# A hybrid attention and mixture-of-experts layer: the first expert's rows selected by matmul, the router summed by quarters, the norm's scale and shift applied apart, the early weight slots split six and six

## The chip, the core and the metric

The kernel runs on one core of one Trainium2 chip, written in Bass with a tile framework whose scheduler sets the order of each engine's instructions. A core has TensorE (matmul, "PE" in the profile, with the load of its stationary operand as "PEld"), VectorE ("DVE"), ScalarE ("ACT"), GpSimd ("POOL") and SyncE ("SP", which here only issues DMAs), 16 DMA engines, SBUF (128 partitions) and PSUM (the matmul's accumulators). Each engine works through its own instructions in order, and semaphores tie them together. The metric is the device time of one execution in microseconds (us).

## What is computed

One layer on 512 tokens of width 1024, float32. The attention part ends in an output projection; the residual is normed, a router picks 4 of 32 experts for each token, the experts' outputs are added with their gates, and a second norm follows. The part of the reference that the change touches:

```python
x = _layer_norm(alpha * x + mix, ln1_g[l], ln1_b[l])       # mix: attention heads @ w_out
ffn = _moe(x, router_w[l], router_b[l], w_gate_up[l], b_gate_up[l], w_down[l], b_down[l])
x = _layer_norm(alpha * x + ffn, ln2_g[l], ln2_b[l])
...
def _layer_norm(x, g, b):                                   # (x - mu) * rsqrt(var + eps) * g + b
...
logits = (xf @ router_w + router_b)                         # in _moe
top_v, top_e = lax.top_k(logits, TOP_K)
gate_w = jax.nn.softmax(top_v, axis=-1)
...                                                         # per expert e, with its tokens' rows:
h = x_pad[tk] @ w_gu[e] + b_gu[e]
glu = gate * jax.nn.sigmoid(gate * SWIGLU_ALPHA)            # gate, up: clipped halves of h
y = ((up + 1.0) * glu) @ w_dn[e] + b_dn[e]
```

## The kernel before

**Weights of the experts.** Each expert has 12 pieces of 1 MB: eight of the gate-and-up matrix ("gu", one for each k of 128 input columns) and four of the down matrix ("dn"). `order` lists all 384; `fetch` (L78) brings the next one into a slot of the ring (tile `wring`). There are 18 slots in three pools, opened as SBUF comes free: `NA = (7, 3, 8)`. `prefetch` fills slots that have not been used yet; afterwards `ring` (L1110) issues the next fetch each time a piece is taken up, and that DMA waits until TensorE is done with what lay in the slot. All these DMAs stand in SP's queue.

**End of the attention part.** The output projection runs over four quarters q of 256 columns and four blocks t of 128 tokens (`product` L727, three matmuls for each pair of heads because the operands are split into a high and a low part). `residual` adds it to `x1all` and takes statistics. `turn` (L687) transposes two 128-column pieces of `x1all` for each quarter and block and copies them to `x1t`. In the last quarter `close(t)` takes the mean and the variance, and `router` (L698) makes the logits: eight matmuls `lp` from the eight stored pieces, corrected afterwards by the norm's factors (`fold`, L671, has folded the norm's scale and shift into the router's weights). `pick` (L831) finds the top four (`MAX8`, index, one-hot `oh`, sum `mf`, mask `msk`), TensorE counts the tokens ahead (`pp`), and `pos` gives each token's place in each expert's list. `norm` (L709) writes the normed block in place, each half either by ScalarE and two POOL instructions ("p") or by two VectorE instructions ("v"), and stores the block to DRAM (`x1d`), from where rows are gathered.

**From the list to the first matmul.** `routing.first` (L897) makes expert 0's list of row numbers: comparison of slot numbers with `pos` (`a0`), 12 small matmuls (`ip`), three VectorE instructions (`rows`). In `moe`, `gather` (L1007) clears the buffers `xg` and fetches an expert's rows from `x1d` by three indirect DMAs on POOL; `transposed` (L1015) turns them by TensorE to `xt`, six transposes and two copies. `gate_up` (L1042) multiplies them into the accumulator `gu`, after a bias matmul from `bpart`: for four pieces k the first two of three groups of 32 list places, then the third group of the same four, then the next four pieces. From expert 1 on the third group is skipped if the expert has at most 64 tokens. `act` is the activation (five instructions), `down` (L1079) the second matmul, after which ScalarE applies the gates and POOL adds the rows to `accd` in DRAM by indirect DMAs.

**Order of experts.** Before expert 0's matmuls the kernel gathers the rows of experts 0, 1 and 2 (`begin`, with `plan` making the lists of the next experts: `places` on VectorE, 12 small matmuls `ixp` for each expert). After them follow `start_sum` (the down biases weighted by the gates, 16 matmul instructions `ip` from `bd`, and the store of the scaled residual to `accd`) and `count`. Then, for each expert e: transposes of the previous expert's hidden rows (`at`), `gate_up` of e, transposes of the rows of e + 1, `down` of e - 1, `act` of e. The tail reads `accd` back, norms and stores.

## Time and profile before

| | |
|---|---|
| timed runs | 1452.08, 1453.5, 1456.73 us, median 1453.5 |
| profiled execution | 1447.06 us |
| its span, first to last instruction | 1445.3 us |
| mean granted TensorE clock | 0.968 |
| TensorE busy | 1303.5 us (90%) |
| VectorE, ScalarE, POOL busy | 413.2, 303.0, 391.4 us |
| moved by DMA | 454.17 MB, mean 314 GB/s |
| weight pieces | 384 of 1 MB, median 21 us from issue to landing |

Lines of code are those of the kernel before (L12 is line 12). A row in order of time gives the start, the length, the engine, the line, the operation, what is written "<-" from what is read, and how many like instructions the row merges; in brackets stands the idle time of the engine ahead of it and what ended that. The granted clock is a share of 2.4 GHz: 1.00 is that, 0.50 is 1.2 GHz. The DMA share is the mean busy share of the 16 DMA engines; it can come out a little above one.

### The profile page before, as it was taken

Reading aid. Unit: us, or ns where it says so; the run is one execution under the profiler, and the core shown is the slowest. Engines: PE = TensorE matmul, PEld = TensorE weight load, DVE = VectorE, ACT = ScalarE, POOL = GpSimd, SP = SyncE. Lnnn points to the kernel's source line nnn. Section 1 sums busy time; section 2 is a strip of 40 time slices with the busy share of each in tenths; the row PEclk is TensorE's granted clock in tenths of the full one; section 3 lists DMA queues with packets and bytes.
Section 4 is the critical chain, followed back from the end, with each engine's and each line's share of the span. In section 5 each row is a group of like instructions: output and inputs, shape, how many; then the busy total and the mean of one; then the engine's idle time right before and its main releaser. Section 6 shows DMA issues by size and latency. Waiting matters only on the chain. (4 is left out here: it accounts for less than half of the span.)

```text
span 1445.3 us, 31835 instructions
## 1 busy us (share of the span) xinstructions
PE 1303.5 (90%) x13903; PEld 672.3 (47%) x13904; DVE 413.2 (29%) x888; ACT 303.0 (21%) x683; POOL 391.4 (27%) x331
## 2 busy tenths in 40 slices
PE   8999899994999999899999999999899898998980
PEld 6777667893243443444343343444334333344340
DVE  3576464647212212222121212122121212001114
ACT  4475265641011011111111111111111111101111
POOL 5333333335103132132221213132331313131124
PEclk9999999996899999999999999999999999999996
DMA  8210113546889999999999999999999999999973
GB/s 220 81 34 1 48 44 124 205 161 253 314 317 393 371 396 403 400 405 406 399 410 401 407 392 408 405 401 402 393 403 397 399 397 409 392 402 386 407 256 127
DMA packets 126260, 454.17 MB, mean 314 GB/s; under 512 B 21416, under 2 KB 53642, under 8 KB 93334
## 3 DMA queue, kind: packets, MB, share of 16 engines
q1 hardware_dynamic: 107526, 435.00, 76.4%
q0 software_dynamic: 18432, 16.84, 5.6%
q8 instruction: 126, 2.06, 0.6%
q14 instruction: 32, 0.26, 0.0%
q10 hardware_dynamic: 144, 0.00, 0.0%
HBM read 441.26 MB, written 18.87 MB: 318 GB/s over the span
## 5 line engine op out<-in xcount | busy, mean ns | idle before, releaser
L1048 PE MATMUL gu<-wring,xt 128*32 128x512 f32 x5312 | 588.8, 595 | 16.9 <-DMA wring<-in_w_gate_up_dram 10.5
L1048 PEld LDWEIGHTS gu<-wring,xt 128*32 128x32 f32 x5312 | 181.3, 110 | 398.7 <-issue 351.2
L1087 PE MATMUL ya<-wring,at 128*32 128x256 f32 x5312 | 312.9, 387 | 8.0 <-DMA wring<-in_w_down_dram 3.6
L1104 POOL DMA_INDIRECT accd<-y,ix x96 | 151.1, 1574 | 487.6 <-ACT y L1103 464.4
L1070 DVE TENSOR_SCALAR ga<-gu 128x768 f32<-128x768 f32 x32 | 30.6, 958 | 778.5 <-PE gu L1048 506.7
L1087 PEld LDWEIGHTS ya<-wring,at 128*32 128x32 f32 x5312 | 171.1, 111 | 138.4 <-issue 35.4
L1010 POOL DMA_INDIRECT xg<-x1d,ix x96 | 101.6, 1058 | 327.9 <-PE ya L1087 156.2
L1021 ACT COPY xt<-tp 128x512 f32<-128x512 f32 x64 | 27.6, 482 | 562.9 <-PE gu L1048 304.7
L173 POOL TENSOR_TENSOR wl<-raw,wh 128x1024 fp32r<-128x1024 f32 (+2 forms) x28 | 67.9, 2430 | 94.8 <-ACT wh L170 91.2
L1103 ACT ACTIVATE y<-ya,gw 128x256 f32<-128x256 f32 x96 | 38.6, 473 | 209.9 <-PE ya L1087 123.4
L1020 PE MATMUL tp<-ident,ga 128*128 128x128 f32 x192 | 34.1, 291 | 40.5 <-DVE ga L1076 38.6
L880 DVE TENSOR_TENSOR places<-slot,pos 128x1536 bf16<-128x1536 bf16 x31 | 54.3, 1753 | 54.6 <-PE ixp L890 54.6
L1021 ACT COPY at<-tp 128x512 f32<-128x512 f32 x64 | 30.2, 481 | 133.2 <-PE tp L1020 133.2
L244 PE MATMUL pjt<-xh,wh 128*128 128x512 f32 (+1 forms) x136 | 52.8, 388 | 0.8 <-DVE xl L222 0.8
L1020 PEld LDWEIGHTS tp<-ident,ga 128*128 128x128 f32 x192 | 21.9, 143 | 68.1 <-issue 68.1
L244 PE MATMUL pjt<-xh,wl 128*128 128x512 f32 (+1 forms) x136 | 52.4, 385 | 0.0
L244 PE MATMUL pjt<-xl,wh 128*128 128x512 f32 (+1 forms) x136 | 52.1, 383 | 0.0
L170 ACT CAST wh<-raw 128x1024 fp32r<-128x1024 f32 (+2 forms) x28 | 29.5, 1054 | 52.9 <-issue 23.5
L1074 ACT ACTIVATE sg<-ga 128x768 f32<-128x768 f32 x32 | 27.0, 845 | 41.4 <-DVE ga L1070 37.8
L430 ACT ACTIVATE pr<-pr,nm 128x256 f32<-128x256 f32 (+3 forms) x64 | 33.8, 529 | 7.5 <-DVE nm L429 6.9
L1020 PE MATMUL tp<-ident,xg 128*128 128x128 f32 x192 | 28.8, 286 | 6.6 <-DMA xg<-x1d,ix 6.6
L1048 PE MATMUL gu<-bpart,bsel 96*32 96x512 bf16 x332 | 29.7, 389 | 3.5 <-DVE up L1072 3.2
(324 smaller groups left out, 1320.4 us busy)
## 6 DMA issues: line engine op xcount, KB each, us to landing
wring<-in_w_gate_up_dram SPq DMA_DIRECT2D x256, 1024.0 KB, 21.1
wring<-in_w_down_dram SPq DMA_DIRECT2D x128, 1024.0 KB, 21.4
raw<-in_w_in_dram SPq DMA_DIRECT2D x16, 512.0 KB, 3.9
raw<-in_w_out_dram SPq DMA_DIRECT2D x8, 512.0 KB
x1all<-in_x_dram SPq DMA_DIRECT2D x4, 512.0 KB, 7.6
x1d<-x1all SPq DMA_DIRECT2D x4, 512.0 KB
accd<-x1all SPq DMA_DIRECT2D x4, 512.0 KB
x1all<-accd SPq DMA_DIRECT2D x4, 512.0 KB, 6.4
```

Source lines behind the costliest of these rows:

```text
L173: eng.tensor_tensor(l[:, :m], raw[:, :m], h[:, :m].bitcast(FT), op=OP.subtract)
L244: nc.tensor.matmul(ps[:, qs], a[:, k, :], b[:, k, qs], start=(k == 0 and n_ == 0), stop=(k == 7 and n_ == 2))
L430: nc.scalar.activation(pr[:, :n], pr[:, :n], AF.Exp, bias=nm, scale=-1.0, accum_out=den)
L880: ins = self.nc.vector.tensor_tensor(a, self.slot[:, None, :].to_broadcast([P, n, NG * P]), pos[:, :, None].to_broadcast([P, n, NG * P]), ...
L1010: nc.gpsimd.indirect_dma_start(out=xg[:, g * 256:(g + 1) * 256], out_offset=None, in_=x1d, in_offset=bass.IndirectOffsetOnAxis(ap=ix[g], a ...
L1020: nc.tensor.transpose(pt[:, u * P:(u + 1) * P], src[:, (a + u) * P:(a + u + 1) * P], ident)
L1021: nc.scalar.copy(dst[:, a:a + n], pt[:, :n * P].rearrange("p (u q) -> p u q", q=P))
L1048: nc.tensor.matmul(ps[SL * c:SL * (c + 1), g, :], lhs(g), w[:, c * 512:(c + 1) * 512], start=start, stop=stop)
L1070: nc.vector.tensor_scalar(ga, v[:, :, :, 0], 7.0, None, op0=OP.min)
L1087: nc.tensor.matmul(ya[SL * c:SL * (c + 1), g, :], listed(at, k, g), w[:, k % 2, c * 256:(c + 1) * 256], start=(k == 0 and g % 2 == 0), sto ...
L1103: nc.scalar.activation(y[:, cs], ya[:, g, :], AF.Copy, scale=gw[g])
L1104: sc.append(nc.gpsimd.indirect_dma_start(out=accd, out_offset=bass.IndirectOffsetOnAxis(ap=ix[g], axis=0), in_=y[:, cs], in_offset=None, b ...
```

## The change

1. **Slots.** `NA = (6, 6, 6)`: still 18 slots, but 12 of them open before the last quarter. Attention's probability tiles move out of the pool `work` into pools of their own (`heads`), which are closed after the attention heads, so the second ring pool has room for six. The first six pieces are fetched ahead of the loads of the gate biases, six more in two lots of three in quarters 1 and 2, the last six after the last product.
2. **Router by quarters.** `turn` multiplies its two transposed pieces at once into a PSUM tile `lp` that all quarters share; `fold` therefore runs before the projection. `router` only reads the sum.
3. **Norm apart.** ScalarE writes (x - mean) / deviation for both halves; scale and shift follow as two instructions for each half on POOL or VectorE (`scaled`, `NORM1`), after the selection has read the block.
4. **First expert's rows.** `pick` makes a one-hot `oh0` of token against place for expert 0; `select` multiplies it with the normed block, eight matmuls for each block into two PSUM tiles. The result is already transposed; `first_rows` applies scale and shift in eight ScalarE instructions and writes `xt`. `routing.first`, expert 0's gather and its transposes are gone. All four blocks are stored to `x1d` after block 3 is scaled.
5. **Expert 0's matmuls** go piece by piece with all three groups, and the lists of experts 0 to 3, the gathers of experts 1 and 2, `start_sum` and `count` are put between the pieces.
6. **Later experts.** The transposes of the hidden rows stand in the middle of the next expert's `gate_up` instead of ahead of it.

```diff
-NA = (7, 3, 8)
-EARLY = (2, 1, 1)
-MORE = 1
+NA = (6, 6, 6)
+NORM1 = ["pp", "pp", "pv", "vv"]
...
-            pr = work.tile([P, S], FT, name="pr", tag="pr", bufs=6)
+            pr = hpool.tile([P, S], FT, name="pr", tag="pr", bufs=6)
...
+    env["prefetch"](NA[0])
     for i in range(NT):
         k0 = max(0, i - 1) * P
...
     swa.close()
+    heads.close()
     env["ring_pool"](NA[1])
...
     def turn(t, q):
...
-        nc.scalar.copy(x1t[t][a][:, k0:k0 + 2], pt[:, :256].rearrange("p (k q) -> p k q", k=2))
+        x1t = work.tile([P, 2, P], FT, name="x1t", tag="x1t", bufs=2)
+        nc.scalar.copy(x1t, pt[:, :256].rearrange("p (k q) -> p k q", k=2))
+        for k in range(2):
+            nc.tensor.matmul(lp[:, t, :NE], x1t[:, k, :], rw[:, 2 * q + k, :], start=(t == q == k == 0),
+                             stop=(q == 3 and k == 1), skip_group_check=True)
...
+    def select(t):
+
+        if t == 0:
+            picked.extend(psum.tile([P, 4, CAP], FT, name="sel", tag="sc", bufs=3) for _ in range(2))
+        for k in range(8):
+            nc.tensor.matmul(picked[k // 4][:, k % 4, :], x1all[:, t, k * P:(k + 1) * P], routing.oh0[:, t, :],
+                             start=(t == 0 and k % 4 == 0), stop=(t == NT - 1), skip_group_check=True)
+
+    def first_rows(xt):
+
+        for k in range(8):
+            nc.scalar.activation(xt[:, k % 2::2, SL * (k // 2):SL * (k // 2 + 1)],
+                                 picked[k // 4][:, k % 4, :].rearrange("p (g s) -> p g s", g=NG), AF.Identity,
+                                 scale=gbT[:, 0, k:k + 1], bias=gbT[:, 1, k:k + 1])
+
+    def scaled(t):
         for a in range(2):
             v = x1all[:, t, a * S:(a + 1) * S]
...
+            eng = nc.gpsimd if NORM1[t][a] == "p" else nc.vector
+            eng.tensor_tensor(v, v, gb[0][a], op=OP.mult)
+            eng.tensor_tensor(v, v, gb[1][a], op=OP.add)
...
+    def close(t):
+        turn(t, 3)
...
+        router(t, rs)
+        for a in range(2):
+            v = x1all[:, t, a * S:(a + 1) * S]
+            nc.scalar.activation(v, v, AF.Identity, bias=rs[:, 1:2], scale=rs[:, 0:1])
+        select(t)
+        if t < NT - 1:
+            scaled(t)
+
+    fold()
...
-        if q == 1:
-            env["prefetch"](NA[0])
-        if q == 2:
-            env["prefetch"](NA[1], True)
-            fold()
+        if q in (1, 2):
+            env["prefetch"](NA[1] // 2, True)
...
                 if t == NT - 1:
-                    mixs.close()
                     late.close()
+                    xgb = env["token_pool"]()
                     env["ring_pool"](NA[2])
-                    env["prefetch"](EARLY[0])
+                    env["prefetch"](NA[2], True)
                 if t > 0:
                     close(t - 1)
             close(NT - 1)
-            routing.first(rsm, psum)
+            first_rows(xgb[0].rearrange("p (a q) -> p a q", a=6))
+            scaled(NT - 1)
+            for t in range(NT):
+                nc.sync.dma_start(env["x1d"].rearrange("(s c) d -> s (c d)", c=NQ)[t * P:(t + 1) * P, :],
+                                  x1all[:, t, :])
             routing.gates_of(rsm, work)
...
-        self.places(self.a0[t // 2][:, t % 2:t % 2 + 1], self.pos[:, 0, t:t + 1])
+            self.oh0 = work.tile([P, NT, CAP], FT, name="oh0", tag="q32", bufs=2)[:, :]
+        nc.vector.tensor_scalar(self.oh0[:, t, :].rearrange("p (g s) -> p g s", g=NG),
+                                self.slot.rearrange("p (g c s) -> p g c s", g=NG, c=NQ)[:, :, 0, :],
+                                self.pos[:, 0, t:t + 1], mf[:, 0:1], op0=OP.is_equal, op1=OP.mult)
...
-        for k0 in (0, 4):
+        step = 1 if more is None else 4
+        for k0 in range(0, 8, step):
...
             groups(more, full, lambda: [rows(w, k, range(2, NG)) for k, w in ws.items()])
+            between.get(k0 + step - 1, lambda: None)()
...
-    begin(0)
-    begin(1)
-    begin(2)
...
-    hid = act(gate_up(transposed(xgs.pop(0), "xt", 1), ring("gu", 0), bsel[:, 0:1]))
-    start_sum(start)
-    count()
+    hid = act(gate_up(xgb[0].rearrange("p (a q) -> p a q", a=6), ring("gu", 0), bsel[:, 0:1], None,
+                      {1: lambda: begin(1), 3: lambda: (plan(0), begin(2)), 5: lambda: (start_sum(start), count())}))
...
-        at = transposed(hid, "at", 2)
         if e < NE:
+            at = []
...
-            ps = gate_up(xt, ring("gu", e), bsel[:, e:e + 1], more[e])
+            ps = gate_up(xt, ring("gu", e), bsel[:, e:e + 1], more[e],
+                         {3: lambda: at.append(transposed(hid, "at", 2))})
```

How the order of instructions changes, at three places. First TensorE in the last quarter, around the end of block 2's products (`op`): `pt` are the transposes of block 1, `pp` the count for block 0 and then block 1, `lp` the logits of block 1. Before:

```order
L733 MATMUL op<-wl,mnh 128x256
L733 MATMUL op<-wh,mnl 128x256
L695 MATMUL pt<-ident,x1all 128x128 x2
L847 LDWEIGHTS us
L847 MATMUL pp<-msk,us 128x32
L701 MATMUL lp<-rw,x1t 128x32 x6
L847 LDWEIGHTS on
```

and now:

```order
L866 LDWEIGHTS us
L866 MATMUL pp<-msk,us 128x32
L747 MATMUL op<-wh,mnl 128x256
L747 MATMUL op<-wh,mnh 128x256
L747 MATMUL op<-wl,mnh 128x256
L747 MATMUL op<-wh,mnl 128x256
L700 MATMUL pt<-ident,x1all 128x128 x2
L720 MATMUL sel<-oh_3602,x1all 128x96 x8
L704 MATMUL lp<-rw,x1t 128x32 x2
L866 LDWEIGHTS on
```

The count of block 0 stands ahead of the last products of block 2 instead of behind them, the selection of block 0 is new, and two logits matmuls are left of eight.

Second, TensorE through expert 0's matmuls with the weights (`gu<-wring`); `gp` and `ip` belong to the sum of the down biases, `cp` to the count, `tp` are transposes of gathered rows. Before, from the last list to the sum:

```order
L890 MATMUL ixp<-val,places 128x5
L1020 MATMUL tp<-ident,xg_3866 128x128 x6
L952 MATMUL gp<-ident,gd 128x128
L1048 MATMUL gu<-wring,xt 32x512 x32
L1048 LDWEIGHTS bsel
...
L1048 MATMUL gu<-wring,xt 32x512 x64
L959 MATMUL ip<-bd,gt 128x512 x3
```

and now, from the last list to the rows of expert 1:

```order
L908 MATMUL ixp<-val,places 128x5
L1052 MATMUL gu<-wring,xg_3733 32x512 x16
L957 MATMUL gp<-ident,gd 128x128
L1052 MATMUL gu<-wring,xg_3733 32x512
L964 MATMUL ip<-bd,gt 128x512 x8
L975 LDWEIGHTS on
L975 MATMUL cp<-msk,on 128x32
...
L1052 MATMUL gu<-wring,xg_3733 32x512 x23
L1023 MATMUL tp<-ident,xg_3734 128x128 x6
```

The six transposes ahead of the first weight matmul are gone, and lists, sum and count now stand between the weight matmuls instead of ahead of and behind them.

Third, SP's queue from the tenth piece (before) or the twelfth (now) to the first pieces that need a used slot. Before:

```order
L85 DMA wring<-in_w_gate_up_dram 128x2048 x3
L719 DMA x1d<-x1all 128x1024 x2
L85 DMA wring<-in_w_gate_up_dram 128x2048 x2
L719 DMA x1d<-x1all 128x1024
L85 DMA wring<-in_w_gate_up_dram 128x2048
L719 DMA x1d<-x1all 128x1024
L85 DMA wring<-in_w_gate_up_dram 128x2048 x2
L1130 DMA markd<-xg_3866 1x8
L85 DMA wring<-in_w_gate_up_dram 128x2048
L85 DMA wring<-in_w_down_dram 128x2x1024
L944 DMA bd<-in_b_down_dram 32x512 x8
L85 DMA wring<-in_w_down_dram 128x2x1024 x3
```

and now:

```order
L84 DMA wring<-in_w_gate_up_dram 128x2048 x3
L803 DMA x1d<-x1all 128x1024
L84 DMA wring<-in_w_gate_up_dram 128x2048 x4
L84 DMA wring<-in_w_down_dram 128x2x1024 x2
L803 DMA x1d<-x1all 128x1024 x3
L949 DMA bd<-in_b_down_dram 32x512 x8
L84 DMA wring<-in_w_down_dram 128x2x1024 x2
L84 DMA wring<-in_w_gate_up_dram 128x2048 x4
```

The last six slots stand together behind the store of block 0, and the other three stores behind them; the marker DMA that waited for the first gather is gone.

## Rows read from the trace of the kernel before

**Rows 1.** Windows: stretch, length, busy time of each engine, TensorE clock, DMA share, GB/s.

```profile
307.00:341.00 34.00, 27.78 (x230) 27.12 (x229) 22.15 (x75) 11.76 (x30) 16.18 (x11) 0.91 0.33 122
341.00:364.00 23.00, 6.24 (x78) 3.56 (x82) 16.05 (x39) 1.39 (x4) 11.40 (x10) 0.50 0.73 260
364.00:410.00 46.00, 45.74 (x336) 14.62 (x332) 10.96 (x29) 3.75 (x6) 5.98 (x6) 0.87 0.75 277
410.00:1390.00 980.00, 915.01 (x11028) 389.19 (x11020) 167.35 (x230) 115.02 (x240) 228.09 (x174) 0.99 1.02 399
```

**Rows 2.** SP's queue, waits: who waited for what, us in total, times, longest.

```profile
SPq L85 <- DMA wring<-in_w_gate_up_dram: 221.1, 117, 4.3
SPq L85 <- DMA wring<-in_w_down_dram: 193.2, 90, 3.7
```

**Rows 3.** Order of time, SP's queue, 220 to 560 us: start, length, DMA issued, count.

```profile
250.27 0.40 SPq L605 DMA_DIRECT2D raw<-in_w_out_dram  x1
251.10 4.17 SPq L85 DMA_DIRECT2D wring<-in_w_gate_up_dram  x5
...
284.41 0.98 SPq L85 DMA_DIRECT2D wring<-in_w_gate_up_dram  x2
...
297.84 1.37 SPq L85 DMA_DIRECT2D wring<-in_w_gate_up_dram  x3
...
331.04 1.71 SPq L85 DMA_DIRECT2D wring<-in_w_gate_up_dram  x2
...
408.00 1.19 SPq L85 DMA_DIRECT2D wring<-in_w_gate_up_dram  x2
```

**Rows 4.** Order of time, TensorE, 318 to 420 us.

```profile
318.90 1.42 PE L701 MATMUL lp<-rw,x1t 128*128 128x32 f32 x12
...
325.93 0.18 PE L847 MATMUL pp<-msk,us 128*128 128x32 bf16 x1 [2.03 <-DVE msk L844]
...
332.22 0.38 PE L695 MATMUL pt<-ident,x1all 128*128 128x128 f32 x2
...
348.89 1.04 PE L1048 MATMUL gu<-bpart,bsel 96*32 96x512 bf16 x8 [0.26 <-DVE v L874]
350.96 0.48 PE L890 MATMUL ixp<-val,places 128*128 128x5 bf16 x12 [1.03 <-DVE places L880]
...
362.82 0.66 PE L1020 MATMUL tp<-ident,xg 128*128 128x128 f32 x2 [5.11 <-DMA xg<-x1d,ix]
...
363.62 9.65 PE L1048 MATMUL gu<-wring,xt 128*32 128x512 f32 x64
...
387.16 1.98 PE L959 MATMUL ip<-bd,gt 32*128 32x512 f32 x6
...
399.78 7.07 PE L1048 MATMUL gu<-wring,xt 128*32 128x512 f32 x64
```

**Rows 5.** Order of time, VectorE, 295 to 420 us.

```profile
321.39 0.75 DVE L717 SCALAR_TENSOR_TENSOR x1all<-x1all,mv,gb 128x512 f32<-128x512 f32 x1
...
335.91 1.53 DVE L717 SCALAR_TENSOR_TENSOR x1all<-x1all,mv,gb 128x512 f32<-128x512 f32 x1
...
342.73 0.21 DVE L851 COPY pos<-pp 128x32 f32<-128x32 f32 x1
342.98 0.56 DVE L880 TENSOR_TENSOR a<-slot,pos 128x384 bf16<-128x384 bf16 x1
...
344.76 0.16 DVE L911 TENSOR_TENSOR ix<-inv,v 128x3 int32<-128x3 f32 x1
```

**Rows 6.** Order of time, POOL, 290 to 470 us.

```profile
335.43 1.46 POOL L715 TENSOR_TENSOR x1all<-x1all,gb 128x512 f32<-128x512 f32 x1
...
350.97 2.73 POOL L1010 DMA_INDIRECT xg<-x1d,ix  x1 [0.18 <-POOL xg L1005]
```

**Rows 7.** Order of time, ScalarE, 268 to 312 us.

```profile
283.50 1.05 ACT L170 CAST wh<-raw 128x1024 fp32r<-128x1024 f32 x1 [2.03 <-PE op L733]
...
298.87 0.37 ACT L696 COPY x1t<-pt 128x256 f32<-128x256 f32 x1
```

More of the change, by code (lines that the diff above doesn't have):

```diff
@@ L101, in x1_pool, with token_pool @@
                 p.tile([G, NE], BF, name="bsel"))
+    def token_pool():
+        p = ctx.enter_context(tc.tile_pool(name="xgp", bufs=1, side="left", reuse_waits="tile"))
+        return [p.tile([P, 768], FT, name=f"xg{i}") for i in range(3)]
     def prefetch(n=NE, pin=False):
@@ L494, in attention @@
     nsx.close()
+    mix_fs = late.enter_context(tc.tile_pool(name="mix_fs", bufs=1, side="right", reuse_waits="tile"))
+    hpool = pool(heads, "heads")
     fox = ExitStack()
@@ L683, in fold @@
         nc.vector.tensor_tensor(rw, rw, gbT[:, 0, :, None].to_broadcast([P, 8, NE]), op=OP.mult)
[L685 removed]
+    lp = psum.tile([P, NT, P], FT, name="lp", tag="ot", bufs=1)
     def turn(t, q):
[L688 to L691 removed]
         pt = psum.tile([P, S], FT, name="pt", tag="pt")
@@ L698, in router @@
     def router(t, rs):
-        lp = psum.tile([P, S], FT, name="lp", tag="sc", bufs=3)
-        for k in range(8):
-            nc.tensor.matmul(lp[:, :NE], x1t[t][k // 4][:, k % 4, :], rw[:, k, :], start=(k == 0), stop=(k == 7))
         lg = small.tile([P, NE], FT, name="lg", tag="lg")
         nc.vector.scalar_tensor_tensor(lg, rsum, rs[:, 1:2], rb, op0=OP.mult, op1=OP.add)
-        nc.vector.scalar_tensor_tensor(lg, lp[:, :NE], rs[:, 0:1], lg, op0=OP.mult, op1=OP.add)
+        nc.vector.scalar_tensor_tensor(lg, lp[:, t, :NE], rs[:, 0:1], lg, op0=OP.mult, op1=OP.add)
@@ L980, in count @@
         nc.vector.tensor_scalar(thr, cnt, float(2 * SL), None, op0=OP.is_gt)
-    bases = [1] + list(range(2, NE, 2))
-    ixs, gwt = ({0: [v[:, 0, g:g + 1] for g in range(NG)]} for v in (routing.ix0, routing.gw0))
+    bases = [0, 1] + list(range(2, NE, 2))
+    ixs, gwt = {}, {}
     def plan(e0):
@@ L1000, in plan @@
             gwt[e0 + e] = [gw[:, e, g:g + 1] for g in range(NG)]
-    xgb = []
-    for i in range(3):
-        xb = rt.tile([P, 768], FT, name=f"xg{i}")
-        nc.gpsimd.memset(xb, 0.0)
-        xgb.append(xb)
+    for i in (1, 2):
+        nc.gpsimd.memset(xgb[i], 0.0)
     def gather(ix, i):
@@ L1040, in groups, with gate_up @@
                 part()
-    def gate_up(xt, weights, pick, more=None):
+    def gate_up(xt, weights, pick, more=None, between={}):
         ps = gups
@@ L1054, in rows @@
             column_tiles(lambda g: listed(xt, k, g), w, False, k == 7, gs)
-        for k0 in (0, 4):
+        step = 1 if more is None else 4
+        for k0 in range(0, 8, step):
             ws = {}
             def full():
-                for k in range(k0, k0 + 4):
+                for k in range(k0, k0 + step):
                     ws[k] = weights(k).rearrange("p a c -> p (a c)")
@@ L1146, in moe @@
             more[e] = third(e)
-            ps = gate_up(xt, ring("gu", e), bsel[:, e:e + 1], more[e])
+            ps = gate_up(xt, ring("gu", e), bsel[:, e:e + 1], more[e],
+                         {3: lambda: at.append(transposed(hid, "at", 2))})
             if e + 1 < NE:
                 xt = transposed(xgs.pop(e + 1), "xt", 1)
-        down(at, ring("dn", e - 1), ixs[e - 1], gwt[e - 1], more.pop(e - 1, None))
+        else:
+            at = [transposed(hid, "at", 2)]
+        down(at[0], ring("dn", e - 1), ixs[e - 1], gwt[e - 1], more.pop(e - 1, None))
         if e < NE:
```

80 lines of the change are left out of this document (18 added, 62 removed).

## Prediction

> **What bounds the kernel now.** I first read the table of stages. From 410 to 1390 us the DMA share is 1.02 at 399 GB/s: for two thirds of the span the 16 DMA engines never rest [rows 1]. The waits of the queue that issues the weight slots agree: SP held a slot back 207 times, 414 us in all, because earlier slot transfers were still under way [rows 2]. TensorE is busy for 915 of those 980 us, close, but it is not what sets the pace. So the end is the moment at which the weight stream becomes continuous, plus a fixed amount of weight, plus a tail that the change leaves alone. A slot costs about 2.74 us: 358 of the 384 are issued between 408.00 and the end of that stretch (982 / 358) [rows 1, 3].
>
> Then I looked at what makes the stream start late. From 307 to 341 us the DMA share is 0.33, from 341 to 364 it is 0.73, from 364 to 410 it is 0.75 [rows 1]. The last two are 6.2 + 11.5 = 17.7 us of idle DMA. All ten early slots are issued by 297.84, the other eight follow from 331.04 on, and then the ring is full: a further transfer needs a slot that TensorE has used up. The first weight matmul runs at 363.62, 31.4 us behind the last product of the output projection (332.22), and the first slot that expert 1 frees goes out at 408.00, another 44.4 us later [rows 3, 4]. In between stands the detour of expert 0's rows: index list ready at 344.76 [rows 5], gather issued at 350.97 [rows 6], its last piece transposed at 362.82 after a wait of 5.11 us [rows 4]. The change replaces exactly this detour, so I cost it as a shift of the first weight matmul.
>
> **Step 1: TensorE up to the last product (332.22 now).** The logits' matmuls of the first three quarters move ahead: 3 quarters x 4 blocks x 2 = 24, in two passes each, 48 instructions. Twelve of these took 1.42 us [rows 4], 0.118 each: +5.7 us. TensorE fills this stretch completely (the output projection runs without holes), so it is paid in full. Blocks 0 and 1 need 12 fewer each in the last quarter: 24 x 0.118 = -2.8. The row selection of blocks 0 and 1 is new: 2 x 8 matmuls in two passes, 32 instructions; the trace has no such shape, the nearest are the logits (0.118) and the transposes (2 in 0.38): +3.8, and twice that at the low clock. The wait of 2.03 us for block 0's mask [rows 4] now has 16 product matmuls in front of it: I take half of it away, -1.0. Each early logits pair waits for a ScalarE copy of 0.37 us [rows 7], and at about six of the twelve places only one to four products stand between: 6 x 0.3 = +1.8. Sum +7.5: the last product ends near 339.7 (bounds 336, if copies and mask are hidden, and 343, if selection runs at half clock).
>
> **Step 2: from the last product to the first weight matmul (31.4 us now).** The chain to the last block's positions stays: 342.73 - 332.22 = 10.5 [rows 4, 5]; its logits are 12 instructions shorter per block, up to -2.8. Behind it come one multiply or add of block 2's half on VectorE, which now stands between the positions and the one-hot (0.75, as the row at 321.39), the one-hot itself (about 0.25, a quarter of the columns of the 0.56 us row at 342.98, plus fixed cost), the last selection (16 x 0.118 = 1.9, or 3.8 at the low clock; the clock was 0.50 over 341 to 364, so I take 3.0) and the bias matmuls (1.04). ScalarE's eight scalings (0.37 each as the copy) run half beside the selection and half beside the bias. Sum 10.5 + 0.75 + 0.25 + 3.0 + 1.04 = 15.5, less half a us for the shorter logits: 15. Bounds: 12.3 and 18.7. First weight matmul at 339.7 + 15 = 354.7, which is 8.9 earlier (bounds 15.3 and 1.9).
>
> A half that VectorE does while POOL does the other one can be slow. The same kind of VectorE instruction took 0.75 us at 321.39 and 1.53 at 335.91, where POOL had begun its 1.46 us instruction at 335.43 [rows 5, 6]. The Trainium skill (SBUF — State Buffer, Who interferes with whom) says that a VectorE instruction with two SBUF inputs and a GpSimd instruction that reads SBUF lock each other out, "whoever issues first gets the shared pair for the whole instruction"; the two rows agree. The change puts such a pair exactly there: both halves of block 2 are released by the same selection. If POOL wins, two VectorE instructions wait some 0.8 us each and the gain is 1.5 us smaller; that lies within the bounds above.
>
> **Step 3: from there to the stream.** Before, 44.4 us passed to the first slot of expert 1. Now TensorE also makes four index lists in this time, 0.48 each [rows 4]: +1.9; the six transposes of the hidden rows leave it, about -1.0; and the bias of expert 1 follows the last matmul of expert 0 at once, where the activation's two reads hold it up: 0 to 2, I take 0.5. The sum over the down biases (within the 12.6 us from 387.16 to 399.78) moves between two matmuls of expert 0 and costs the same. Net +1.4, so the shift that reaches the stream is 8.9 - 1.4 = 7.5; with the clock already raised by the selection it may be 8. I take **8**.
>
> Does the DMA keep up? At about 340 it owes six slots (16.4 us), the stored rows and the down biases (2.6 MB, 6.6 us at 399 GB/s): done near 363, when expert 0 has begun to free slots. It frees them one by one, 24 matmuls of 0.11 each (64 in 7.07 us), 2.65 us a slot against 2.74: the stream follows. Before expert 1's first four slots a hole of some 5 us is left (11.5 now). So the stream is still led by TensorE there, and the shift is what counts, not the whole 17.7.
>
> **What costs nothing, and its cover.** The first six slots stand ahead of the gate biases on SP: those are due at the bias matmuls (348.89), far behind. The third load of the output weights (250.27 now) falls behind a bias load that waits for the moved fold; its cast is at 283.50 [rows 3, 7], some 10 us of cover after it lands; without them it would hold the second half of a quarter. The store of block 0 stands on SP ahead of the last six slots; it needs POOL's four instructions after the first selection, about 339, when the last product frees the room anyway. Those slots are the third half-dozen: expert 0's eight are in the first twelve. Rows of experts 1 and 2 are gathered beside expert 0's matmuls; they are due after about 30 us. The fold moves, its price doesn't. From expert 4 on TensorE's order is as it was.
>
> **The sum.** The profiled execution took 1447.06 us (span 1445.3): 1447.1 - 8 = 1439.1. The three timed runs lie 6.4 us higher (median 1453.5); the same shift gives **1445.5**.
>
> **The rivals.**
> *More* (0.16): selection and logits fall into waits that TensorE has anyway, and the clock holds. First weight matmul at 336 + 12.3 = 348.3, 15.3 earlier, less 1.4: about 1439.5. For it: 2.03 us of waiting and a clock of 0.91 in 307 to 341. Against: the products before that run without a gap.
> *Too little to see* (0.24): selections at half clock, VectorE locked out, casts ahead of the copies: 342 + 17.2 = 359.2, 4.4 earlier, less 1.4: 1450.5.
> *Slower* (0.10): TensorE works in order, so a late ScalarE copy now holds the products behind each early logits pair, and ScalarE does the gate-bias casts in the same stretch. If each of the twelve pairs waits 1.6 us instead of the 0.15 in my sum, step 1 grows by 17: 1453.5 + 9 = 1462.5. It decides from 0.8 us each on (gain gone); slower than 0.3% from 1.2 on. Against it: the order puts 4 to 11 products behind most pairs.
> *The shift is not passed on* (in the 0.24): if the stream were held by something other than freed slots after 364, it would not move. Against it: its DMA idles there.
>
> **How the numbers follow.** Forecast 0.50, with its own range 1441 to 1449. The measurement tells about 0.3% (4.4 us) from no change: forecast and "more" are faster, 0.66; too little 0.24; slower 0.10. Low end 1437 holds most of "more"; the high end 1453 takes in "too little" and leaves the slow case out.
>
> **What would show it.** Right: first weight matmul near 355; no gather before it; the low-DMA stretch ends with the last product and the share from 341 to 400 is above 0.9; expert 1's first freed slot near 400; 1.02 after that. Step 1 is wrong if the last product of the projection is not near 340 (see TensorE's waits for ScalarE copies); step 2 if the first weight matmul is not 15 us behind it; step 3 if matmuls of expert 0 wait for index lists, gathers or weights. The whole is wrong if the continuous stretch has another rate than 399 GB/s.

## The result and the profile after

The changed kernel takes 1460.3 us (median of 18 runs, 1455.6 to 1471.2), the kernel before 1452.1 (18 runs, 1446.9 to 1458.5): ratio 1.0066, 95% interval 1.0044 to 1.0088. It is 8 us slower, where 8 us less were forecast. Ratios here and below are taken over the fast runs, and are not quotients of the medians. The profiled execution took 1456.1 (span 1454.4), 9.1 more than that of before.

The stages of the changed kernel, answering [rows 1] (stretch, length, busy time of PE, PEld, DVE, ACT and POOL, TensorE clock, DMA share, GB/s):

```profile
307.00:341.00 34.00, 30.26 (x251) 29.35 (x251) 16.47 (x49) 13.13 (x28) 11.32 (x8) 0.99 0.41 156
341.00:364.00 23.00, 17.66 (x90) 14.60 (x93) 12.05 (x42) 7.10 (x19) 7.55 (x6) 0.50 0.89 333
364.00:410.00 46.00, 44.87 (x393) 14.99 (x389) 24.37 (x52) 3.85 (x6) 9.28 (x9) 0.96 0.72 269
410.00:1390.00 980.00, 913.35 (x10956) 398.50 (x10949) 168.04 (x230) 115.33 (x240) 231.76 (x174) 0.98 1.02 397
```

The waits of SP's queue in the long stretch, answering [rows 2], and TensorE's and VectorE's waits that grew:

```profile
SPq L84 <- PE gu L1052: 167.2, 51, 9.9
SPq L84 <- PEq L1042: 156.4, 31, 11.2
SPq L84 <- PE ya L1093: 146.1, 34, 14.1
SPq L84 <- DMA wring<-in_w_gate_up_dram: 131.6, 73, 3.2
SPq L84 <- DMA wring<-in_w_down_dram: 102.9, 47, 3.7
...
PE gu L1052 <- DVE up L1078: 12.7, 19, 2.2
...
DVE ix L916 <- DMA accd<-y,ix: 180.8, 13, 15.2
```

The same views of before, beside the two lines of [rows 2]:

```profile
SPq L85 <- PE gu L1048: 101.0, 40, 10.3
SPq L85 <- PE ya L1087: 83.3, 32, 11.4
SPq L85 <- PEq L1039: 76.1, 18, 11.5
...
PE gu L1048 <- DVE up L1072: 3.2, 15, 0.2
```

Before, SP held slots back 414 us for DMAs and 260 for TensorE; now it waits 234 us for DMAs and 470 for TensorE, which frees the slots late. The last line of the first table is new: VectorE's write of an index list waits 180.8 us for a scatter.

**Two losses.** In the stage ahead of the stream the gain is smaller than forecast. TensorE, answering [rows 4]:

```profile
247.10 0.33 PE L747 MATMUL op<-wh,mnh 128*128 128x256 f32 x1
...
331.59 2.02 PE L720 MATMUL sel<-oh,x1all 128*128 128x96 f32 x16
...
339.63 0.18 PE L866 MATMUL pp<-msk,us 128*128 128x32 bf16 x1 [3.73 <-DVE msk L863]
340.53 3.73 PE L720 MATMUL sel<-oh,x1all 128*128 128x96 f32 x16
...
344.54 0.41 PE L747 MATMUL op<-wh,mnl 128*128 128x256 f32 x1
...
356.23 3.70 PE L720 MATMUL sel<-oh,x1all 128*128 128x96 f32 x16 [2.72 <-DVE oh L873]
361.42 1.04 PE L1052 MATMUL gu<-bpart,bsel 96*32 96x512 bf16 x8 [1.49 <-ACT xg L726]
362.22 2.92 PE L1052 MATMUL gu<-wring,xg 128*32 128x512 f32 x16
```

The last product runs at 344.5 (forecast 339.7, bounds 336 to 343), the first weight matmul at 362.2 (forecast 354.7), only 1.4 us before its old time. A part of this is not the change: the projection's first product comes 2.1 us later in this execution. In the profile of before it is this one:

```profile
245.03 0.33 PE L733 MATMUL op<-wh,mnh 128*128 128x256 f32 x1
```

From the projection's first product to the first weight matmul it takes 115.1 us, 118.6 before: 3.5 less. One execution of each is a coarse measure of that. Run 3 below, the kernel before with an edit behind this stretch, takes 123.3; runs 1, 2, 7, 8, 9 and 16, the changed kernel with edits behind it or none, take 112.8 to 115.2.

What is lost in this stage shows in the same piece: TensorE waits 3.73 us for block 1's mask, and then selects at half clock (3.73 us for the 16 instructions that took 2.02 for block 0). VectorE and POOL in that time, answering [rows 5, 6]:

```profile
333.25 0.88 DVE L762 SCALAR_TENSOR_TENSOR rs<-mv,rs 128x1 f32<-128x1 f32 x1 [0.60 <-ACT rs L761]
334.22 1.31 DVE L709 SCALAR_TENSOR_TENSOR lg<-rsum,rs,rb 128x32 f32<-128x32 f32 x1
335.97 0.77 DVE L857 CAST idf<-i 128x4 f32<-128x4 uint32 x1
337.42 2.15 DVE L863 CAST msk<-mf 128x32 bf16<-128x32 f32 x1
...
353.52 1.56 DVE L734 TENSOR_TENSOR x1all<-x1all,gb 128x512 f32<-128x512 f32 x1 [2.15 <-PE pp L866]
...
332.86 1.26 POOL L734 TENSOR_TENSOR x1all<-x1all,gb 128x512 f32<-128x512 f32 x1 [16.09 <-ACT x1all L766]
334.20 1.29 POOL L735 TENSOR_TENSOR x1all<-x1all,gb 128x512 f32<-128x512 f32 x1
...
336.80 1.39 POOL L735 TENSOR_TENSOR x1all<-x1all,gb 128x512 f32<-128x512 f32 x1
338.13 1.41 POOL L1008 MEMSET xg<- 128x768 f32 x2
```

Four instructions of 0.15 to 0.25 us (their times one block earlier) take 0.8 to 2.2 and end each time when a POOL instruction ends. The trace of before has such a case already, which the rows of the prediction leave out: a 128x1 instruction of 0.16 us (L767) took 1.02 from 322.28, until POOL's multiplication (321.48, 1.80 us) had ended.

The second loss lies in the stream. From 600 to 900 us (same columns; before, then after):

```profile
600.00:900.00 300.00, 281.64 (x3414) 121.81 (x3406) 54.51 (x76) 34.81 (x72) 73.71 (x58) 1.00 1.03 403
...
600.00:900.00 300.00, 274.89 (x3228) 119.09 (x3224) 50.63 (x69) 34.80 (x72) 72.91 (x57) 0.96 1.01 392
```

11 GB/s over 300 us are 3.3 MB, 8 us at 399 GB/s: as much as the whole difference. VectorE's activations (the read of `gu`, one per expert) come at the same times up to expert 6 (0.5 us earlier than before), 17.1 us later by expert 15, and 7.0 us later at the last expert. One boundary, expert 7, first before (VectorE, then TensorE), then after:

```profile
608.30 0.96 DVE L1070 TENSOR_SCALAR ga<-gu 128x768 f32<-128x768 f32 x1 [24.97 <-PEq L1039]
...
619.65 0.17 DVE L911 TENSOR_TENSOR ix<-inv,ixv 128x6 int32<-128x6 f32 x1
...
610.19 0.64 PE L1048 MATMUL gu<-bpart,bsel 96*32 96x512 bf16 x8
612.33 0.74 PE L1020 MATMUL tp<-ident,ga 128*128 128x128 f32 x5 [1.49 <-DVE ga L1076]
...
615.00:620.00 5.00, 5.00 (x95) 3.21 (x94) 4.17 (x8) 0.37 (x1) 0.00 (x0) 1.00 1.01 411
```

```profile
610.57 0.17 DVE L916 TENSOR_TENSOR ix<-inv,ixv 128x6 int32<-128x6 f32 x1 [15.20 <-DMA accd<-y,ix]
610.66 0.95 DVE L1076 TENSOR_SCALAR ga<-gu 128x768 f32<-128x768 f32 x1
...
612.53 0.61 PE L1052 MATMUL gu<-bpart,bsel 96*32 96x512 bf16 x8 [2.21 <-DVE up L1078]
614.68 1.30 PE L1023 MATMUL tp<-ident,ga 128*128 128x128 f32 x5 [1.53 <-DVE ga L1082]
...
610.00:615.00 5.00, 1.26 (x18) 0.47 (x10) 3.82 (x5) 0.84 (x1) 2.86 (x3) 0.84 1.01 421
615.00:620.00 5.00, 5.00 (x40) 2.46 (x39) 0.00 (x0) 0.60 (x2) 3.74 (x4) 0.50 1.02 398
```

The list for experts 10 and 11 stood behind expert 7's activation; now it stands ahead of it. It is written over the list of experts 4 and 5 (three buffers), and expert 5's scatter, issued at 598.45, still reads that one. VectorE works in order, so the activation waits with it, the next bias matmuls wait 2.21 us for the activation, and TensorE's clock falls to its lower level. In 5 of the 13 places the activation follows directly; in the others the wait ends 4 to 9 us ahead of it. TensorE's own order has hardly changed here: from 555 us on both traces have the same weight matmuls and transposes in the same order, those of the hidden rows (`tp<-ident,ga`) too, and only the lists' small matmuls (`ixp`) stand one expert earlier.

### The profile page after: what moved, and what is told of

Its sections match the earlier page's. It is cut to its first block, busy times and chain, and to the rows that moved or that the text cites. A ratio compares the mean times of both kernels' runs of the same rounds, so it can differ in the third digit from the quotient of the medians.

```text
span 1454.4 us, 31908 instructions
## 1 busy us (share of the span) xinstructions
PE 1322.8 (91%) x13949; PEld 697.0 (48%) x13950; DVE 415.6 (29%) x888; ACT 307.1 (21%) x692; POOL 387.4 (27%) x327
## 3 DMA queue, kind: packets, MB, share of 16 engines
q8 instruction: 126, 2.06, 0.6%
## 5 line engine op out<-in xcount | busy, mean ns | idle before, releaser
L1052 PE MATMUL gu<-wring,xt 128*32 128x512 f32 x5120 | 562.6, 592 | 8.5 <-PEq L1042 6.6
L1093 PE MATMUL ya<-wring,at 128*32 128x256 f32 x5312 | 320.6, 394 | 5.8 <-PEq L1042 2.8
L1013 POOL DMA_INDIRECT xg<-x1d,ix x93 | 98.5, 1059 | 191.4 <-issue 143.0
L1024 ACT COPY xt<-tp 128x512 f32<-128x512 f32 (+1 forms) x62 | 26.7, 482 | 519.5 <-PE gu L1052 296.6
L916 DVE TENSOR_TENSOR ix<-inv,ixv 128x6 int32<-128x6 f32 (+1 forms) x17 | 2.9, 168 | 180.8 <-DMA accd<-y,ix 180.8
L1052 PE MATMUL gu<-bpart,bsel 96*32 96x512 bf16 x332 | 28.1, 387 | 15.5 <-DVE up L1078 13.8
```

Source lines behind the costliest of these rows:

```text
L1013: nc.gpsimd.indirect_dma_start(out=xg[:, g * 256:(g + 1) * 256], out_offset=None, in_=x1d, in_offset=bass.IndirectOffsetOnAxis(ap=ix[g], a ...
L1024: nc.scalar.copy(dst[:, a:a + n], pt[:, :n * P].rearrange("p (u q) -> p u q", q=P))
L1052: nc.tensor.matmul(ps[SL * c:SL * (c + 1), g, :], lhs(g), w[:, c * 512:(c + 1) * 512], start=start, stop=stop)
L1093: nc.tensor.matmul(ya[SL * c:SL * (c + 1), g, :], listed(at, k, g), w[:, k % 2, c * 256:(c + 1) * 256], start=(k == 0 and g % 2 == 0), sto ...
```

## The experiments

Theory A: the lists moved one expert ahead cost the 8 to 10 us. Rivals: B, the clock falls because the transposes of the hidden rows stand elsewhere; C, the loss is made ahead of 410 us. For what is lost ahead of the stream, D: POOL holds the mask back; E: the mask's chain starts late. For what a gain there is worth, F (passed on in full), G (in part), H (not). Times are medians; each ratio is to the kernel before on the same chip.

| run | edit | us | before there | ratio, interval |
|---|---|---|---|---|
| 1, 8, 16 | five list buffers | 1450.5, 1451.2, 1450.9 | 1453.7, 1453.8, 1451.4 | 0.9986, 0.9980, 0.9995 (0.995 to 1.002) |
| 2, 9 | transposes back | 1449.5, 1451.8 | 1453.7, 1453.8 | 0.9974, 0.9989 (0.994 to 1.002) |
| 3 | before, transposes moved | 1462.8 | 1453.7 | 1.0064 (1.0032 to 1.0096) |
| 4 | scale and shift written later | 1461.6 | 1453.7 | 1.0059 (1.0028 to 1.0090) |
| 7 | changed kernel again | 1461.9 | 1453.8 | 1.0068 (1.0041 to 1.0095) |
| 5 | transposes back, scale held off | 1466.0 | 1482.2 | 0.9916 (0.9882 to 0.9949) |
| 6 | five buffers, scale held off | 1453.8 | 1482.2 | 0.9827 (0.9775 to 0.9879) |
| 10, 15 | the same | 1449.1, 1448.7 | 1453.8, 1451.4 | 0.9959, 0.9969 (0.993 to 0.999) |
| 11, 13 | before, start delayed | 1493.9, 1466.4 | 1478.5, 1451.4 | 1.0121 (1.0076 to 1.0165), 1.0090 (1.0061 to 1.0118) |
| 12, 14 | run 6, start delayed | 1466.5, 1457.1 | 1478.5, 1451.4 | 0.9924 (0.9897 to 0.9952), 1.0041 (1.0020 to 1.0062) |

Runs 5, 6, 11 and 12 fell on chips that run the kernel before some 25 to 28 us slower; between chips only ratios are compared. Two things there stay unexplained: runs 5 and 6 lie 12.2 us apart, though their two cures differ by 0.6 us in runs 8 and 9, and run 6 gains 1.7 per cent, where the same kernel gains 0.3 to 0.4 in runs 10 and 15.

### The lists

Run 1:

```
-        ix = rt.tile([P, n, NG], I32, name="ix", tag="ix", bufs=3)
-        gw = rt.tile([P, n, NG], FT, name="gw", tag="gw", bufs=3)
+        ix = rt.tile([P, n, NG], I32, name="ix", tag="ix", bufs=5)
+        gw = rt.tile([P, n, NG], FT, name="gw", tag="gw", bufs=5)
```

> The changed kernel, with five buffers instead of three for the index lists and the gates of two experts; the order of the instructions stays. Theory A (lists too early): since the change VectorE makes each list one expert earlier, and its write of the list waits 11 to 15 us (180.8 us in 13 places) for the scatter that still reads the list in that buffer; VectorE works in order, so five activations come some 2.2 us late and TensorE idles behind them. Then the waits of the list writes are gone (180.8 to under 10 us), TensorE's wait ahead of the bias matmuls falls from 12.7 us to about 3, and the time to 1449 to 1455 us (before 1452.1, changed kernel 1460.3). Theory B (clock): TensorE's clock falls at the expert boundaries because the transposes of the hidden rows now stand elsewhere; then the list waits go, but the mean clock stays near 0.963 and the time at 1458 to 1462. Theory C (head): the loss is made ahead of 410 us; time 1458 to 1462 as well, with the experts 7 to 15 as fast as in the kernel before (31.3 us each).

Run 2 (the last expert's `else` goes with it):

```
+        at = transposed(hid, "at", 2)
         if e < NE:
-            at = []
...
-            ps = gate_up(xt, ring("gu", e), bsel[:, e:e + 1], more[e],
-                         {3: lambda: at.append(transposed(hid, "at", 2))})
+            ps = gate_up(xt, ring("gu", e), bsel[:, e:e + 1], more[e])
```

> The changed kernel, with the transposes of the hidden rows written ahead of the next expert's gate-and-up matmuls again, as before; nothing else undone. Its list writes stand one expert later again on VectorE, behind the same activation as in the kernel before. Theory A: list waits gone, SP waits more for its own DMAs than for TensorE again, experts 7 to 15 in about 31.3 us each, time 1446 to 1454 us. Theory B (the place of the transposes alone, through the clock) expects the same time here, 1446 to 1454, but no gain from more list buffers. Theory C (head): 1458 to 1462, nothing gained.

Run 3 is the reverse of that edit, in the kernel before (`gate_up` gets the argument `between` with it):

```
-        at = transposed(hid, "at", 2)
         if e < NE:
+            at = []
...
-            ps = gate_up(xt, ring("gu", e), bsel[:, e:e + 1], more[e])
+            ps = gate_up(xt, ring("gu", e), bsel[:, e:e + 1], more[e],
+                         {3: lambda: at.append(transposed(hid, "at", 2))})
```

> The kernel before, with one part of the change alone: the transposes of the hidden rows are written behind the first half of the next expert's gate-and-up matmuls. The lists of experts 8 and up come one expert earlier on VectorE with it. Theories A and B: slower than before by 5 to 9 us, 1457 to 1461, with list writes that wait for scatters (A: over 100 us of such waits). Theory C (head): no change, 1450 to 1454.

Runs 7, 8 and 9 put the changed kernel and the first two edits on one chip:

> The changed kernel unaltered, to stand on one chip beside the three that follow, since the fifth and sixth experiments ran on a chip where the kernel before took 1482 us instead of 1453. All theories: slower than the kernel before by 0.4 to 0.9 per cent on the same chip, with list waits of about 180 us on VectorE.

> The first experiment again (five list buffers) on one chip with the others. Theory A: 7 to 11 us below the changed kernel, within 0.3 per cent of the kernel before. Rival (the gain of the first experiment came from the chip or from chance): within 3 us of the changed kernel.

> The second experiment again (transposes back) on one chip with the others: 8 to 12 us below the changed kernel by theory A. If the chip decides, the two cures differ by more than 5 us here, as the fifth and the sixth did on their chip.

The three waits of run 8 (five buffers), where 12.7 us, 131.6 and 102.9 stood, and no list write waits for a scatter any more; then VectorE's list waits of run 3:

```profile
PE gu L1052 <- DVE up L1078: 3.2, 15, 0.2
...
SPq L84 <- DMA wring<-in_w_gate_up_dram: 213.1, 109, 3.6
SPq L84 <- DMA wring<-in_w_down_dram: 165.4, 77, 4.7
...
DVE ix L911 <- DMA accd<-y,ix: 172.5, 12, 15.2
```

Five buffers leave the order as it is and bring 10.7 us on one chip (1461.9 to 1451.2); moving the transposes back restores the order and brings 10.1. That excludes B: runs 1, 8 and 16 leave the transposes where they are, and in the traces of the two kernels they stand at the same place there. It excludes C as the cause of the loss. The move alone costs the kernel before 9 us (run 3), with the same waits. A is shown. The edit of five buffers holds for the gates `gw` too, whose writes stand ahead of the lists' and waited 44.7 us for ScalarE; the two waits go together and are not told apart. The same runs show what the rest of the change is worth: 1, 8 and 16 are the changed kernel without the list waits, and equal the kernel before within 0.2 per cent, with an interval that holds 1.

### The mask

Run 4 called block t's scale and shift one block later. The scheduler put them back: POOL's first multiplication still follows directly on block 0's selection, and the same five VectorE instructions take 0.88, 1.32, 0.77, 2.15 and 1.51 us. It says nothing on D or E.

```
         select(t)
-        if t < NT - 1:
-            scaled(t)
+        if 0 < t < NT - 1:
+            scaled(t - 1)
...
+            scaled(NT - 2)
```

> The changed kernel, with the scale and shift of blocks 0, 1 and 2 each one block later (behind the next block's selection, block 2's behind the last eight scalings). Theory D: the mask of block 1 is 3.7 us late because POOL multiplies and adds block 0 in 332.9 to 338.2 and VectorE's small instructions wait for it (0.88, 1.31, 0.77, 2.15 and 1.51 us for instructions of 0.15 to 0.3). Then these take under 0.4 us, TensorE's wait of 3.73 us goes, the clock stays up there, the last product ends at 339 to 341 instead of 344.5 and the first weight matmul runs at 355 to 358 instead of 362.2. The time falls by 0 to 4 us only if the stream is led from there, to 1456 to 1460. Rival E: the mask is late because its chain starts late; then the last product stays at 344 and the time at 1460.

So the later start was made a matter of data. `after(t)` is a column of ones computed from the one-hot of block t; the multiplications of blocks 0, 2 and 3 also multiply by one:

```
-NORM1 = ["pp", "pp", "pv", "vv"]
+NORM1 = ["vv", "pp", "vv", "vv"]
...
+    def after(t):
+        one = small.tile([P, 1], FT, name="one", tag="one", bufs=2)
+        nc.vector.tensor_scalar(one, routing.oh0[:, t, 0:1], -1.0, None, op0=OP.is_ge)
+        return one
...
+                eng.scalar_tensor_tensor(v, v, one, gb[0][a], op0=OP.mult, op1=OP.mult)
...
+        if t == 1:
+            scaled(0, after(1))
+            scaled(1)
...
+            one = after(NT - 1)
+            for t in range(2, NT):
+                scaled(t, one)
```

> The changed kernel with the transposes of the hidden rows as before (the edit of the second experiment), and the scale and shift held off by data: block 0's and then blocks 2's and 3's are done by VectorE, each multiplication also by a column of ones that is made from the one-hot of block 1 (for block 0) or of block 3 (for blocks 2 and 3), so POOL has block 1 alone. Theory D (POOL's multiplications hold VectorE's mask back): the mask instructions of block 1 take 0.15 to 0.4 us again, TensorE's wait for that mask falls from 3.7 to under 1 us, and from the last quarter's first transposes of block 0 to the first weight matmul it takes 27 to 31 us instead of 35.0 (44.9 in the kernel before). Theory E (the mask's chain starts late): the wait stays at 2.5 us or more. On the time: if the stream is led by TensorE from there on, 4 to 6 us less than the second experiment (1449.5), so 1443 to 1446; if the ring is full and the early slots decide, no change, 1448 to 1451.

> The same holding-off of scale and shift, but with five list buffers instead of the transposes moved back (the edit of the first experiment). Both cures take the list waits away, so the time should stand to the first experiment (1450.5) as the fifth stands to the second: 1444 to 1447 if TensorE leads the stream from 364 us on, 1449 to 1452 if not.

TensorE in run 6, from block 0's mask on, and the cast of block 1's mask on VectorE:

```profile
329.05 0.18 PE L877 MATMUL pp<-msk,us 128*128 128x32 bf16 x1
...
334.34 0.18 PE L877 MATMUL pp<-msk,us 128*128 128x32 bf16 x1
335.54 2.02 PE L720 MATMUL sel<-oh,x1all 128*128 128x96 f32 x16 [0.23 <-DVE oh L884]
...
343.38 0.18 PE L877 MATMUL pp<-msk,us 128*128 128x32 bf16 x1 [2.06 <-DVE msk L874]
...
354.85 3.65 PE L1063 MATMUL gu<-wring,xg 128*32 128x512 f32 x16
...
334.11 0.18 DVE L874 CAST msk<-mf 128x32 bf16<-128x32 f32 x1
```

Block 1's mask is there without a wait, its cast takes 0.18 us instead of 2.15, the selection runs at full clock (2.02), and from block 0's mask to the first weight matmul it takes 25.8 us, against 31.5 in the changed kernel (330.69 to 362.22) and 37.7 in the kernel before (325.93 to 363.62; 39.6 in run 3). D holds, and E does not: the mask comes 5.3 us behind block 0's instead of 8.9. A wait of 2.06 is left at block 2, where POOL works on block 1. The edit also moves block 2's multiplication off the way; of the 5.7 us, 5.2 lie between block 0's mask and the last product (8.6 instead of 13.8), 0.5 behind it.

### What an earlier start is worth

> The sixth experiment again (five list buffers, scale and shift held off) on one chip with the others. If TensorE leads the stream from 364 us on: 4 to 6 us below the first edit alone, that is 1444 to 1447 on a chip where the kernel before takes 1453. If the early slots decide: within 2 us of the first edit alone.

A delay can be dosed more purely than a gain. In runs 11 and 13 (the kernel before) and 12 and 14 (run 6), TensorE does 110 transposes that nobody reads, ahead of expert 0. The edit of runs 12 and 14 (runs 11 and 13 transpose the gathered rows, `xgs[0]`, ahead of expert 0's own six transposes):

```
+    for _ in range(110):
+        nc.tensor.transpose(pst.tile([P, 512], FT, name="idle", tag="tr")[:, :P], xgb[0][:, :P], ident)
     hid = act(gate_up(xgb[0].rearrange("p (a q) -> p a q", a=6), ring("gu", 0), bsel[:, 0:1], None,
```

> The kernel before, with 110 transposes of gathered rows of expert 0, whose result nobody reads, on TensorE right ahead of expert 0's own six transposes: the first weight matmul comes some 15 to 18 us later, nothing else is changed. Theory F (the premise of the prediction: the stream is led by the first weight matmul, a shift there is passed on in full): the time rises by 13 to 18 us, to 1.009 to 1.012 of the kernel before. Theory G (the shift is passed on by about 0.3, as the steps from 44.9 over 35.3 to 28.9 us between last quarter and first weight matmul gave 1453.8, 1451.5 and 1449.1 us): up by 4 to 6 us, 1.003 to 1.004. Theory H (the ring is full and the start does not matter): under 2 us.

> The kernel of the sixth and tenth experiments (five list buffers, scale and shift held off), with the same 110 transposes, of expert 0's selected rows, ahead of expert 0's bias matmuls: its first weight matmul is put back to about where the kernel before has it (44 to 46 us behind the last quarter's first transposes instead of 28.9). Theory F: 14 to 17 us above the tenth experiment, 1.005 to 1.008 of the kernel before on the same chip. Theory G: 4 to 6 us above it, 0.999 to 1.001 of the kernel before. Theory H: as the tenth, 0.996.

> The eleventh experiment again (the kernel before with 110 transposes ahead of expert 0, first weight matmul 16 to 18 us later), beside the three that follow. On a chip where the kernel before takes 1478 us it rose by 15.4 us. On a chip where it takes 1453 us, as in the profile: theory F (passed on in full) plus 13 to 18 us; theory G (the DMAs lead there most of the way, and a part of the delay is taken up by slots that lie ready) plus 4 to 9 us; theory H under 2 us.

> The twelfth experiment again (five list buffers, scale and shift held off, and the 110 transposes), on one chip with the same kernel without the transposes. F: 14 to 17 us above that kernel; G: 4 to 9; H: under 2.

> The sixth and tenth experiment a third time (five list buffers, scale and shift held off), as the partner of the delayed one on the same chip. Faster than the kernel before by 0.3 to 0.6 per cent on a chip of 1453 us, by 1 to 2 on one of 1480.

> The first and eighth experiment a third time (five list buffers alone), as the partner of the held-off one: its first weight matmul comes 6.4 us later behind the last quarter's first transposes (35.3 against 28.9). F: 5 to 7 us above the partner; G: 2 to 3; H: the same.

The transposes in run 13 and in run 14:

```profile
368.65 15.67 PE L1137 MATMUL idle<-ident,xg 128*128 128x128 f32 x110 [7.60 <-DMA xg<-x1d,ix]
...
352.87 15.59 PE L1143 MATMUL idle<-ident,xg 128*128 128x128 f32 x110 [1.49 <-ACT xg L726]
```

From block 0's mask to the first weight matmul, with the times of the one chip of runs 13 to 16 (the 37.7 is of the profile of before, whose chip is not on record; with the 39.6 of run 3 the first step is 15.4):

| step | mask to first weight matmul | time |
|---|---|---|
| before, then delayed (13) | 37.7 to 55.0: +17.3 | 1451.4 to 1466.4: +15.0 |
| run 15, then delayed (14) | 25.8 to 41.0: +15.2 | 1448.7 to 1457.1: +8.4 |
| run 15, then without holding off (16) | 25.8 to 31.9: +6.1 | 1448.7 to 1450.9: +2.2 |

The ratios of the table above give 13, 10 and 4 us for the same three steps, each with an interval of some 4 us to either side. In the kernel before, a later start is paid for nearly in full, which fits F (13 to 18 us; run 11 gives 15.4 on its chip); from run 15 to run 14 it is 8.4 or 10 us of 15.2, less than F's 14 to 17 and clear of H. The last step, 2.2 or 4 us of 6.1, cannot be told from none. So a shift is passed on in good part, but its share is not settled; that an earlier start counts for less than a later one is suggested by these numbers and not shown. What takes up the rest wasn't isolated: the trace of run 6 shows the DMA share at 0.03 from 396 to 402 and at 0.43 to 0.58 from 492 to 504 us, where the kernel before has one such hole (0.13, 402 to 408). Run 12 decides nothing, as it has no partner on its chip: set beside run 6, on another of the slower chips (0.9827 to 0.9924), the delay costs 14 us, as F has it; set beside run 10 (0.9959) it costs nothing.

Runs 10 and 15 beat both kernels, by 0.3 to 0.4 per cent against the kernel before, with intervals below 1.

## Why the prediction was wrong

**What bounds the kernel** held at most for the kernel before. [rows 2] has its 414 us of waits for DMAs and leaves out the 260 for TensorE, so even there the pace was not the DMA's alone. In the changed kernel the stream has the same share (1.02) but SP waits above all for TensorE; I had noted that TensorE was busy 915 of 980 us and had not asked what a few microseconds more per expert would do. The prediction's last sign, another rate than 399 GB/s in the stream, is the one that came: 397 over all, 392 against 403 from 600 to 900.

**Where it failed first: "From expert 4 on TensorE's order is as it was."** For the weight matmuls and the transposes that is nearly so (from 555 us on, in the traces), but it was taken as a reason to price the later experts at nothing. I looked at TensorE and not at VectorE, and so costed the moved transposes at -1.0 in step 3. Written elsewhere, they let the scheduler take each list one expert ahead, on VectorE, and there the list meets a buffer still being read. This is the added wait that no part of the sum held; it is worth 9 to 11 us (runs 3, 7 to 9), of the 16 between forecast and result. The edit that removes it touches neither transposes nor selection.

**Step 1** (+7.5 to the last product) is +10.4 in the pair of profiles, from the projection's first product to its last (247.10 to 344.54, against 245.03 to 332.10; the 332.22 of the prediction is the transpose behind it). By the kernel before in runs 3, 11 and 13 (89.8 to 91.5 us for 87.1) and the changed kernel in runs 1, 2, 7, 8, 9 and 16 (95.1 to 97.5) it is some 4 to 8. So the size may have been right, which is luck, as two terms were not. The mask was missized: half of the 2.03 wait should have gone (-1.0), it grew to 3.73 (+1.7), and the selection behind it ran at half clock: 5.75 us for blocks 0 and 1 instead of 3.8. The selection's price at full clock was right (2.02 for 16, forecast 0.118 each), and the copies cost one wait of 0.54 ahead of the last product (forecast 1.8). The mask's delay is POOL's doing (run 6). I had weighed this for block 2 alone; block 0's scale and shift lie on POOL exactly while VectorE makes block 1's mask, and the held instructions are mostly casts and small ones.

The Trainium skill (SBUF — State Buffer, Who interferes with whom) counts casts, copies and tensor-scalar instructions, when their operands meet certain conditions, among those that can contend with GpSimd for the shared ports, beside those with two SBUF inputs; the cast of 2.15 us instead of 0.18 agrees.

**Step 2** (15 us) measured 17.7, for 31.5 before: the multiplication of block 2, put between positions and one-hot, stood ahead of the positions and took 1.56 instead of 0.75, the addition (0.69) came behind them, the last selection took 3.70 instead of 3.0, and ScalarE's scalings, hidden in my sum, left a wait of 1.49. The sum is within the bounds given (12.3 to 18.7).

**Step 3.** From the first weight matmul to the first slot freed by expert 1 it takes 45.3 us (362.22 to 407.49) against 44.4, so +0.9 where +1.4 stood; that slot goes out half a us earlier than before. But the rule that a shift reaches the end in full, on which the whole sum rests, is too simple: a third to nearly all of one came through, by the medians of runs 13 to 16. Without the list waits the changed kernel is 0.5 to 3.2 us below the kernel before (runs 1, 8 and 16), not 8.

**The rivals.** *Slower* named the time (1462.5) but not the mechanism: the copies of ScalarE cost TensorE 1.0 us in all (0.54, and 0.46 behind the last product). *Too little to see* describes the change without its list waits: first weight matmul 359.2 forecast, 362.2 measured, and ratios of 0.998 to 0.9995 in runs 1, 8 and 16. *The shift is not passed on* came true in part (runs 14 and 15). That the order of another engine moves far from the edit was no rival, and should have been one.

## What to carry to other kernels

Where a scheduler orders the engines, compare the order on every engine over the whole program, also far from the edit: an instruction that comes earlier on an in-order engine may meet a buffer that is still in use, and hold up everything behind it. When an engine's work is moved from VectorE to POOL, look at what VectorE does in those microseconds, down to its smallest instructions. What an earlier start is worth is best measured by delaying it, with its partner on the same chip: a dose on TensorE that nobody reads costs a few lines. Read a stage from an event at its own start and in several executions: the profiles of one code here differ by 14 us in where the projection begins.

## What the runs showed of the hardware

- A scatter that adds 128 rows of 1 KB took some 12 us from its issue (598.45) until VectorE was let go (610.57), under the full weight stream; the page of the profile gives a median of 10.6 from issue to landing. A list's buffer is in use that much longer than POOL's own instruction (1.56).
- VectorE instructions of 0.15 to 0.3 us took up to 2.15 beside POOL's multiplications, and two MEMSETs of POOL (338.13) held a tensor-scalar instruction too (1.51 instead of 0.29); in run 6 the same one took 0.86 beside the MEMSETs (334.18).
- TensorE idled 2.21 us ahead of 612.53 and 1.53 ahead of 614.68, and was then at 0.50 of its clock, the lower level, from 615 to 620; in the kernel before it idled 1.49 at the same place and the clock stayed at 1.00. In the 300 us where this repeats the mean clock is 0.96 against 1.00, by estimate 12 us of TensorE's work; with five buffers (run 8) it is 0.98.
- With the changed kernel's attention part, seven of 14 profiles (runs 1, 2, 4, 8, 9, 10, 15) have a TensorE clock of 0.84 to 0.89 from 180 to 245 us and begin the projection at 253.9 to 258.8; all seven profiled executions lie above the median of their run. The other seven have 1.00 and begin at 245.0 to 248.0, the four with the attention part of before at 244.9 to 246.8, with 1.00 too. Whether the change brings the low clock more often, and loses time by it, was not tested.
- Of the four chips on record, two ran the kernel before in 1478 and 1482 us, the other two in 1451 to 1454. Only the traces from the first two (runs 5, 6, 11 and 12) have waits of SP's queue that the profile puts down to nothing on the core (`remote`), 7.9 to 80.5 us from 410 to 1390.
